# Modulation steps tied to TensorE's three waits at each LayerNorm boundary, and the two moment sums in a PSUM bank each

## The chip, the cores and the metric

The kernel runs on one core of one Trainium2 chip. Its engines are TensorE (PE in the profile; PEld is its weight load), VectorE (DVE), ScalarE (ACT), GpSimd (POOL) and SyncE (SP), which issues the loads. The metric is the device time of one execution in microseconds, the median of several runs.

## What is computed

One denoising step of a two-layer backbone in float32, for 128 context tokens and 256 latent tokens of width 1024. Each layer has three sub-layers: a SwiGLU feed-forward, a mixer (latent attention beside a gated recurrence, joined by one output product) and a second feed-forward. All three have the same frame:

```python
h = x * (1 + m[1]) + m[0]
x = layer_norm(ALPHA * x + 0.5 * m[2] * swiglu(h, w_up, w_down), ln_g, ln_b)
h = x * (1 + m[4]) + m[3]
y, aux = mixer(h)
x = layer_norm(ALPHA * x + m[5] * y, ln_g, ln_b)
h = x * (1 + m[7]) + m[6]
x = layer_norm(ALPHA * x + 0.5 * m[8] * swiglu(h, w_up2, w_down2), ln_g, ln_b)
```

The nine vectors `m` of a layer are the modulation: SiLU of a conditioning vector times a 1024 by 9216 matrix, once for the context tokens and once for the latent ones. They depend on no token, so their products can be done at any time before their first use; their weights are 72 MB in all.

## The kernel before

**Layout.** The residual stream `X` is kept transposed: eight chunks of 128 features on the partitions, 384 tokens along the free axis. A float32 product is made of three matmuls of reduced-precision parts (`mm3`, L317): a weight tile `ws` is split by ScalarE (`wh`, L313) and VectorE (`wl`, L314), the input by `split_affine` (L273) into `hh` and `hl`. Each of the three lines L318 to L320 is one 128x128 by 128x384 matmul.

**The modulation pump.** `Pump` cuts the modulation products into steps. One step takes a tile `wm` of 1 MB (three buffers, loaded by SP at L189). A group of `by_tensor` does a step as matmuls with 32 output rows on TensorE (L236); a group of `by_vector` sums on VectorE (L248, L250) and leaves a small matmul. When a group's last step is done, `finish` turns the result by a VectorE transpose (L228) and adds a bias (L229). `PUMPED` is the order of the groups, `MIX_STEPS` and `NEXT_STEPS` say how many steps are traced at the mixers and at the boundaries.

**The boundary.** `Residual.add` (L345) takes a finished output chunk `c`: two VectorE instructions put it into `X` (L349), ScalarE squares it (L354), GpSimd adds it to the running sums of values and of squares (L358, L359). At chunk 6 the sums so far go into PSUM by matmuls with a column of 1/1024 (`columns`, L373), one column a 128-token tile, the means and the mean squares side by side in one bank that a matmul with zeros has cleared (L362); another matmul spreads the mean over all partitions (`pm`, L367). At chunk 7 `moments` (L376) adds the last chunk to all of these (L373, L383); ScalarE squares the mean (L386), VectorE subtracts (L387), GpSimd takes the power -0.5 (L389). `normalise` (L392) transposes the roots into rows `pr` on TensorE (L396), and for each chunk VectorE subtracts and multiplies (L398, L399), after which `split_affine` makes the next input: ScalarE's `hh` (L276) in a context half and a latent half, `h32` by VectorE in even chunks and ScalarE in odd ones (L282, L279), VectorE's `hl` (L284). TensorE's next product needs both halves of `hh`'s first chunk. `next_input` (L451) ties this together for five boundaries; the sixth residual ends the kernel and has no next input.

**Order.** A scheduler orders each engine's instructions by the dependences, its own estimate of times, and a priority, which is the place in the program; `tc.high_priority(offset=n)` moves instructions n places forward. So a step that `next_input` traces may run much earlier or later. Each engine runs its instructions in the order that results. PSUM has three buffers for the small tiles (`misc_tile`: the moments, `pm`, `pr`) and one for the modulation.

## Time and profile before

| | before |
|---|---|
| median of 3 runs | 1615.8 us (1614.57 to 1617.2) |
| span of the profiled execution, first to last instruction | 1610.9 us |
| the profiled execution's own time beside its span | not recorded; the median of the runs stands 4.9 us above the span |
| TensorE busy | 1554.1 us (96% of the span) |
| VectorE, ScalarE, GpSimd busy | 948.3, 659.3, 163.0 us |
| mean granted TensorE clock | 0.984 of full speed |

The profile gives every instruction's start and duration from the start of the span. A row of the timeline names the start, the duration of a run of equal instructions, the engine, the line, the operation, what it writes and reads, and in brackets how long the engine idled before it and what ended that. One matmul of float32 operands stands as two records. Matmuls overlap, so a row's duration is longer than what the next one has to wait; 0.34 us is printed for a product matmul that follows the one before it by 0.17. The granted clock is a share of 2.4 GHz: 0.50 is the lower level, 1.2 GHz.

### The profile page before, as it was taken

The numbers are of one execution on the slowest core, as the hardware profiler recorded it, in microseconds if no ns is written. First come the engines' busy times: TensorE is split into PE (matmuls) and PEld (weight loads), VectorE is DVE, ScalarE is ACT, GpSimd is POOL, SyncE is SP. The second block draws the span as 40 slices with busy tenths as digits, with TensorE's granted clock in tenths as the row PEclk, the third lists the DMA queues.
The fourth block names the chain that finished last, engine by engine and source line by source line (L and its number), as shares of the span: only waits on it lengthen the run. The fifth ranks groups of instructions, "written<-read, shape, count | busy, mean of one in ns | idle before, by whom it ended". The sixth has DMA issues, their size and how long they took to land.

```text
span 1610.9 us, 22640 instructions
## 1 busy us (share of the span) xinstructions
PE 1554.1 (96%) x9106; PEld 1445.0 (90%) x9106; DVE 948.3 (59%) x1556; ACT 659.3 (41%) x1066; POOL 163.0 (10%) x142
## 2 busy tenths in 40 slices
PE   6999999999999899999999999999999989999997
PEld 3899999987668899999989999997867789999996
DVE  2868764477887846873464444345788664444334
ACT  3533333258743533332353333324785444333321
POOL 0000002220004100000220000032010140000012
PEclk8999999999999999999999999999999989999998
DMA  8865653446654545663354334334465214433331
GB/s 305 272 200 175 230 169 126 117 150 207 217 191 132 178 135 182 196 215 120 125 183 134 128 122 133 124 102 164 147 191 202 73 59 131 132 130 120 129 118 40
DMA packets 210596, 249.90 MB, mean 155 GB/s; under 512 B 26298, under 2 KB 185020, under 8 KB 207420
## 3 DMA queue, kind: packets, MB, share of 16 engines
q1 hardware_dynamic: 210492, 248.47, 46.8%
q8 instruction: 71, 1.16, 0.3%
q14 instruction: 33, 0.27, 0.1%
HBM read 245.52 MB, written 1.88 MB: 154 GB/s over the span
## 4 chain that ended last, share of the span: by engine, by line
PE 86%; DVE 5%; issue 3%; DMA 2%; ACT 2%; POOL 1%; SPq 0%; DVEq 0%; POOLq 0%; ACTq 0%
PE acc L318 26%; PE acc L319 26%; PE acc L320 26%; PE gm L236 3%; DMA wm<-in_w_mod_dram 2%; PE acc L745 1%; DVE wl L314 1%; PE ms L373 1%; PE pv L778 1%; PE ms L761 0%; ACT wh L313 0%; DVE hl L284 0%; POOL sum_f L359 0%; DVE tr L866 0%; SPq L189 0%
## 5 line engine op out<-in xcount | busy, mean ns | idle before, releaser
L313 ACT CAST wh<-ws 128x1024 fp32r<-128x1024 f32 (+1 forms) x330 | 335.7, 1019 | 778.3 <-PE acc L319 552.1
L314 DVE TENSOR_TENSOR wl<-ws,wh 128x1024 fp32r<-128x1024 f32 (+1 forms) x330 | 411.1, 1247 | 389.8 <-ACT wh L313 388.7
L318 PE MATMUL acc<-hh,wh 128*128 128x384 f32 x1280 | 428.8, 339 | 7.9 <-ACT hh L276 7.4
L320 PE MATMUL acc<-hh,wl 128*128 128x384 f32 x1280 | 431.9, 338 | 2.9 <-DVE wl L314 2.9
L319 PE MATMUL acc<-hl,wh 128*128 128x384 f32 x1280 | 431.6, 338 | 1.4 <-DVE hl L284 1.4
L318 PEld LDWEIGHTS acc<-hh,wh 128*128 128x128 f32 x1280 | 242.4, 190 | 15.5 <-ACT hh L276 9.0
L320 PEld LDWEIGHTS acc<-hh,wl 128*128 128x128 f32 x1280 | 242.6, 190 | 8.6 <-DVE wl L314 5.5
L319 PEld LDWEIGHTS acc<-hl,wh 128*128 128x128 f32 x1280 | 242.4, 189 | 7.6 <-DVE hl L284 4.4
L318 PE MATMUL acc<-gh,wh 128*128 128x384 f32 x704 | 236.6, 336 | 0.0
L319 PE MATMUL acc<-gl,wh 128*128 128x384 f32 x704 | 236.1, 335 | 0.0
L320 PE MATMUL acc<-gh,wl 128*128 128x384 f32 x704 | 235.9, 335 | 0.0
L318 PEld LDWEIGHTS acc<-gh,wh 128*128 128x128 f32 x704 | 132.2, 188 | 0.4 <-issue 0.4
L319 PEld LDWEIGHTS acc<-gl,wh 128*128 128x128 f32 x704 | 132.3, 188 | 0.0
L320 PEld LDWEIGHTS acc<-gh,wl 128*128 128x128 f32 x704 | 132.2, 188 | 0.0
L481 DVE TENSOR_TENSOR a<-a,acc 128x384 f32<-128x384 f32 x88 | 48.7, 554 | 126.2 <-PE acc L320 125.7
L250 DVE SCALAR_TENSOR_TENSOR gsum<-wm,sil,gsum 128x512 f32<-128x512 f32 x168 | 120.3, 766 | 0.0
L318 PE MATMUL acc<-hh_in,wh 128*128 128x384 f32 x352 | 118.0, 339 | 2.2 <-ACT hh_in L276 2.2
L320 PE MATMUL acc<-hh_in,wl 128*128 128x384 f32 x352 | 117.8, 335 | 0.7 <-DVE wl L314 0.7
L319 PE MATMUL acc<-hl_in,wh 128*128 128x384 f32 x352 | 118.2, 336 | 0.0
L358 POOL TENSOR_TENSOR sum_f<-X 128x384 f32<-128x384 f32 x4 | 5.1, 1282 | 846.3 <-DVE X L349 846.3
L236 PE MATMUL gm<-wm,sil 128*32 128x256 f32 (+1 forms) x512 | 66.2, 532 | 13.0 <-DMA wm<-in_w_mod_dram 11.9
L318 PEld LDWEIGHTS acc<-hh_in,wh 128*128 128x128 f32 x352 | 66.2, 189 | 4.5 <-ACT hh_in L276 3.2
(260 smaller groups left out, 1721.9 us busy)
## 6 DMA issues: line engine op xcount, KB each, us to landing
ws<-in_w_ffn_up_dram SPq DMA_DIRECT2D x88, 1024.0 KB, 5.2
wm<-in_w_mod_dram SPq DMA_DIRECT2D x56, 1024.0 KB, 6.8
ws<-in_w_ffn_down_dram SPq DMA_DIRECT2D x32, 1024.0 KB, 5.0
wm<-in_w_mod_dram SPq DMA_DIRECT2D x32, 512.0 KB, 5.8
ws<-in_w_ffn_down_dram SPq DMA_DIRECT2D x16, 768.0 KB, 4.4
ws<-in_w_in_dram SPq DMA_DIRECT2D x12, 1024.0 KB, 5.4
ws<-in_w_o_dram SPq DMA_DIRECT2D x8, 1024.0 KB, 8.5
ws<-in_w_uq_dram SPq DMA_DIRECT2D x12, 192.0 KB, 3.2
```

The lines of the kernel that those rows point to most:

```text
L236: nc.tensor.matmul(self.ps[32 * g : 32 * g + 32, :n], lhsT, wv[:, g], start=self.fresh, stop=stop)
L250: nc.vector.scalar_tensor_tensor(self.sum[:, r], wv[:, kk], s, self.sum[:, r], op0=ALU.mult, op1=ALU.add)
L313: nc.scalar.copy(parts[0], src)
L314: nc.vector.tensor_tensor(parts[1], src, parts[0].bitcast(F32), op=ALU.subtract)
L318: nc.tensor.matmul(ps, wh, xh, start=start, stop=False)
L319: nc.tensor.matmul(ps, wh, xl, start=False, stop=False)
L320: nc.tensor.matmul(ps, wl, xh, start=False, stop=stop)
L358: nc.gpsimd.tensor_tensor(self.sums[0], X[:, 0, :] if c == 1 else self.sums[0], X[:, c, :], op=ALU.add)
L373: nc.tensor.matmul(self.pt[:, 2 * i + j : 2 * i + j + 1], src[:, i * P : (i + 1) * P], mean_w[:, 0:1], start=False, stop=stop and i == T / ...
L481: nc.vector.tensor_tensor(a, a, px[:, :T], op=ALU.mult)
L745: nc.tensor.matmul(views[i], qT[hf][0:96, h % 4, q0 : q0 + P], kT[hf][0:96, h % 4, k0:k1], start=True, stop=True)
L778: nc.tensor.matmul(o[:, P:T], v, pTs[e][:, (j - 1) * 256 : j * 256], start=(j == 1), stop=(j == 3))
```

## The change

`next_input` no longer runs its steps at its start. It hands their number to `moments` and `normalise`, which place them by a new function `fill`: a step is traced at high priority, and each of its TensorE instructions is ordered behind a given one (`tc.issue_after`). The first step goes behind the last product's last matmul, the second behind the last column sum of squares, the remaining ones (one, or two at the third boundary) behind the transposes, which become high priority themselves.

The means and the mean squares get one PSUM bank each (two of the three small buffers at that time, so that `pm` takes the third and `pr` waits for the first to be free); each bank is cleared by a matmul with zeros of its own. The mean's column sums and `pm` come first; VectorE copies the mean out of PSUM and squares the copy, where ScalarE squared it; then the column sums of squares follow. In the first chunk of each boundary VectorE makes the context half of `hh` (`swift`). The last tensor group of two vectors, (1, 7) and (1, 8), becomes two groups of one. In the result's `finish` the copy of the mean is the one that `moments` makes. The rest of the diff removes comments.

```diff
@@ PUMPED
-          + by_vector((1, 1), (1, 3), (1, 4)) + by_tensor((1, 2)) + by_tensor((1, 5), (1, 6)) + by_tensor((1, 7), (1, 8)))
+          + by_vector((1, 1), (1, 3), (1, 4)) + by_tensor((1, 2)) + by_tensor((1, 5), (1, 6)) + by_tensor((1, 7))
+          + by_tensor((1, 8)))
@@ split_affine
-            nc.scalar.activation(hh[:, c, t0:t1], X[:, c, t0:t1], AF.Identity,
-                                 bias=B[:, c, r : r + 1], scale=G[:, c, r : r + 1])
+            if swift and r == 0:
+                nc.vector.tensor_scalar(hh[:, c, t0:t1], X[:, c, t0:t1], G[:, c, r : r + 1], B[:, c, r : r + 1],
+                                        op0=ALU.mult, op1=ALU.add)
+            else:
+                nc.scalar.activation(hh[:, c, t0:t1], X[:, c, t0:t1], AF.Identity,
+                                     bias=B[:, c, r : r + 1], scale=G[:, c, r : r + 1])
@@ mm3
-        nc.tensor.matmul(ps, wl, xh, start=False, stop=stop)
+        newest["product"] = nc.tensor.matmul(ps, wl, xh, start=False, stop=stop)
+
+    def fill(ins, n=1):
+
+        with tc.high_priority(offset=CHAIN_AHEAD), tc.issue_after(ins.ins):
+            pump.step(n)
@@ Residual.add
-                    self.pt = misc_tile()
-                    nc.tensor.matmul(self.pt[:, :6], mean_w, zeros, start=True, stop=False)
+                    self.pt = [misc_tile() for _ in range(2)]
                     for j in range(2):
+                        nc.tensor.matmul(self.pt[j][:, :3], mean_w, zeros[:, :3], start=True, stop=False)
                         self.columns(j, self.sums[j])
@@ moments
-        def moments(self):
+        def moments(self, fills=0):
+
             name = self.name
+            if fills:
+                fill(newest["product"])
             with tc.high_priority(offset=CHAIN_AHEAD):
-                self.columns(0, self.tail[0])
-                self.columns(1, self.tail[1], stop=True)
+                self.columns(0, self.tail[0], stop=True)
                 if self.broadcast:
                     nc.tensor.matmul(self.pm[:, :T], mean_w, self.tail[0], start=False, stop=True)
-                mv = self.pt[:, :6].rearrange("p (a b) -> p a b", b=2)
+                mean = tmp.tile([P, 4], F32, tag="v4", name=f"mean_{name}")
+                nc.vector.tensor_copy(mean[:, :3], self.pt[0][:, :3])
                 m2 = tmp.tile([P, 4], F32, tag="m2", name=f"m2_{name}")
-                nc.scalar.activation(m2[:, :3], mv[:, :, 0], AF.Square)
-                nc.vector.scalar_tensor_tensor(m2[:, :3], mv[:, :, 1], LN_EPS, m2[:, :3], op0=ALU.add, op1=ALU.subtract)
+                nc.vector.tensor_tensor(m2[:, :3], mean[:, :3], mean[:, :3], op=ALU.mult)
+                last = self.columns(1, self.tail[1], stop=True)
+                nc.vector.scalar_tensor_tensor(m2[:, :3], self.pt[1][:, :3], LN_EPS, m2[:, :3], op0=ALU.add, op1=ALU.subtract)
...
+            if fills > 1:
+                fill(last)
+            return mean, rs
@@ normalise
-            _, rs = self.moments()
+            _, rs = self.moments(fills)
             pm, pr = self.pm, misc_tile()
-            for i in range(3):
-                nc.tensor.matmul(pr[:, i * P : (i + 1) * P], rs[:, i : i + 1].to_broadcast([P, P]), ident, start=True, stop=True)
+            with tc.high_priority(offset=CHAIN_AHEAD):
+                for i in range(3):
+                    last = nc.tensor.matmul(pr[:, i * P : (i + 1) * P], rs[:, i : i + 1].to_broadcast([P, P]), ident,
+                                            start=True, stop=True)
+            if fills > 2:
+                fill(last, fills - 2)
@@ next_input
-        pump.step(steps)
         pump.finish()
...
-        for c in res.normalise():
-            split_affine(hh, hl, c, G, B)
+        for c in res.normalise(steps):
+            split_affine(hh, hl, c, G, B, swift=c == 0)
```

## Rows read from the trace of the kernel before

**Rows 1.** The page: its first line, and section 4's shares of the chain by engine.

```profile
span 1610.9 us, 22640 instructions
...
PE 86%; DVE 5%; issue 3%; DMA 2%; ACT 2%; POOL 1%; SPq 0%; DVEq 0%; POOLq 0%; ACTq 0%
```

**Rows 2.** Timeline, first boundary; [ ] is the engine's idle time before.

```profile
318.55 0.34 PE L320 MATMUL acc<-gh,wl 128*128 128x384 f32 x1
...
319.71 0.83 PE L373 MATMUL ms<-mean_w,sum_f 128*128 128x1 f32 x6 [0.26 <-POOL sum_f L359]
...
321.33 0.62 PE L236 MATMUL gm<-wm,sil 128*32 128x256 f32 x2
...
323.73 2.79 PE L236 MATMUL gm<-wm,sil 128*32 128x256 f32 x46
...
324.29 0.88 POOL L389 TENSOR_TENSOR r_f<-m_f,mhalf 128x3 f32<-128x3 f32 x1 [4.63 <-DVE m_f L387]
...
326.45 0.93 PE L396 MATMUL ms<-ident,r_f 128*128 128x128 f32 x6
...
329.44 1.10 PE L318 MATMUL acc<-hh,wh 128*128 128x384 f32 x3 [1.73 <-ACT hh L276]
```

**Rows 3.** Timeline, third boundary.

```profile
820.01 2.79 PE L236 MATMUL gm<-wm,sil 128*32 128x256 f32 x46
...
822.73 0.93 PE L396 MATMUL ms<-ident,r_f 128*128 128x128 f32 x6
...
824.29 1.37 ACT L276 ACTIVATE hh<-X,B,G 128x128 fp32r<-128x128 f32 x3 [4.00 <-DVE X L399]
824.64 0.66 DVE L282 TENSOR_SCALAR h<-X,G,B 128x128 f32<-128x128 f32 x2
...
825.33 0.79 PE L318 MATMUL acc<-hh,wh 128*128 128x384 f32 x3 [1.54 <-ACT hh L276]
```

**Rows 4.** Timeline, second boundary.

```profile
520.72 0.34 PE L320 MATMUL acc<-hh_mix,wl 128*128 128x384 f32 x1
...
520.99 1.06 PE L236 MATMUL gm<-wm,sil 128*32 128x512 f32 x8
...
529.52 0.79 PE L318 MATMUL acc<-hh,wh 128*128 128x384 f32 x3 [0.72 <-ACT hh L276]
```

**Rows 5.** Timeline, fourth boundary.

```profile
1101.98 0.34 PE L320 MATMUL acc<-gh,wl 128*128 128x384 f32 x1
...
1113.40 0.80 PE L318 MATMUL acc<-hh,wh 128*128 128x384 f32 x3 [1.73 <-ACT hh L276]
```

**Rows 6.** Timeline, fifth boundary.

```profile
1305.95 0.34 PE L320 MATMUL acc<-hh_mix,wl 128*128 128x384 f32 x1
...
1309.08 0.17 ACT L386 ACTIVATE m_m<-ms 128x3 f32<-128x3 f32 x1 [1.40 <-PE ms L373]
...
1310.44 1.65 PE L396 MATMUL ms<-ident,r_m 128*128 128x128 f32 x6 [1.40 <-POOL r_m L389]
...
1313.75 1.33 PE L318 MATMUL acc<-hh,wh 128*128 128x384 f32 x3 [1.67 <-ACT hh L276]
```

**Rows 7.** Windows, product matmuls: length, busy (records), clock, DMA share, GB/s.

```profile
329.44:343.00 13.56, 13.07 (x65) 0.87 0.33 141
825.33:839.00 13.67, 12.26 (x67) 1.00 0.59 231
...
1313.75:1328.00 14.25, 14.25 (x66) 0.79 0.00 1
529.52:543.00 13.48, 12.92 (x62) 0.87 0.24 84
300.00:313.00 13.00, 13.00 (x76) 1.00 0.59 151
```

**Rows 8.** Windows, attention: length; PE, PEld, DVE, ACT, POOL busy; clock, DMA, GB/s.

```profile
1220.00:1230.00 10.00, 9.93 (x52) 4.32 (x51) 8.92 (x23) 6.69 (x20) 0.00 (x0) 1.00 0.79 288
```

**Rows 9.** Loads of modulation weights (L189), from issue to landing.

```profile
DMA to landing us min/median/max: 3.7/6.5/12.4
```

More of the change, by code (lines that the diff above doesn't have):

```diff
@@ L271, in load_x, with split_affine @@
             nc.scalar.mul(X[:, c, :], ps[:, :T], ALPHA)
-    def split_affine(hh, hl, c, G, B):
+    def split_affine(hh, hl, c, G, B, swift=False):
         h32 = tmp.tile([P, T], F32, tag="t1", bufs=3, name=f"h32_{n_ps[0]}_{c}")
         for r, (t0, t1) in enumerate(COND):
-            nc.scalar.activation(hh[:, c, t0:t1], X[:, c, t0:t1], AF.Identity,
-                                 bias=B[:, c, r : r + 1], scale=G[:, c, r : r + 1])
+            if swift and r == 0:
[4 more added lines that the diff above has]
+                                     bias=B[:, c, r : r + 1], scale=G[:, c, r : r + 1])
             if c % 2:
@@ L315, in piece @@
         return parts
+    newest = {}
     def mm3(ps, wh, wl, xh, xl, start, stop):
@@ L372, in columns @@
             for i in range(T // P):
-                nc.tensor.matmul(self.pt[:, 2 * i + j : 2 * i + j + 1], src[:, i * P : (i + 1) * P], mean_w[:, 0:1],
-                                 start=False, stop=stop and i == T // P - 1)
-        def moments(self):
+                last = nc.tensor.matmul(self.pt[j][:, i : i + 1], src[:, i * P : (i + 1) * P], mean_w[:, 0:1],
+                                        start=False, stop=stop and i == T // P - 1)
+            return last
+        def moments(self, fills=0):
@@ L397, in normalise @@
+            return mean, rs
+        def normalise(self, fills):
+            _, rs = self.moments(fills)
+            pm, pr = self.pm, misc_tile()
+            with tc.high_priority(offset=CHAIN_AHEAD):
[4 more added lines that the diff above has]
+                fill(last, fills - 2)
             for c in range(KD):
@@ L424, in finish @@
         def finish(self, dsts):
-            mv, rs = self.moments()
-            mean = tmp.tile([P, 4], F32, tag="v4", name=f"mean_{self.name}")
-            nc.vector.tensor_copy(mean[:, :3], mv[:, :, 0])
+            mean, rs = self.moments()
             for i, dst in enumerate(dsts):
```

2 lines of the change are left out of this document (removed).

## The prediction

> **What bounds the kernel now.** I read the page first. The chain that ended last runs on TensorE for 86% of the span [rows 1], and most of that is products of 384 columns that nobody can shorten here; so a change can only pay where TensorE waits or runs slowly. I then asked the timeline for the five stretches between the last product of one sub-layer and the first of the next, numbered 1 to 5 in order of time. Stretch 1 takes 318.55 to 329.44 (10.9 us), 2 takes 520.72 to 529.52 (8.8), 4 takes 1101.98 to 1113.40 (11.4), 5 takes 1305.95 to 1313.75 (7.8); 3 ends at 825.33 [rows 2 to 6]. In each there are three waits of TensorE: for the last chunk's sum on VectorE, for the reciprocal root (GpSimd), and for the first normalised chunk.
>
> What the reader is to see in stretch 1 [rows 2]: the root is done at 324.29 + 0.88 = 325.17, but the transposes that need it start at 326.45, because 46 records of modulation (three steps of 16 less two records, 2.79 us) stand ahead of them in TensorE's order. The work meant to fill a wait outlasts it by 1.3 us. Behind the transposes TensorE then idles 1.73 us with nothing to fill. Stretch 3 has the same block of 46 at 820.01 [rows 3]. Stretch 5 has no modulation at all: its steps ran long before, in the attention.
>
> Last I read the clock, from windows that begin at each first product [rows 7]. Where stretch 3 ends the granted clock is 1.00; after 1 and 2 its mean over 13.5 us is 0.87 and after 5, over 14.25, it is 0.79, so part of those windows ran at the lower level, 1.2 GHz, and the rest at 2.4. In undisturbed products 76 records take 13.00 us, 0.171 us each. By that, what each window loses is: after 1, 13.56 - 65 x 0.171 = 2.4, less a piece of a step like the stray 0.62 of rows 2: 1.8; after 3, 13.67 - 67 x 0.171 = 2.2, less a step (1.06): 1.1; after 5, 14.25 - 66 x 0.171 = 3.0; after 2, 13.48 - 62 x 0.171 = 2.9. For 4, whose code is that of 1, I take 1's. Stretch 3 is the one whose TensorE kept its clock through the boundary; 1.1 us is what the start costs when VectorE and ScalarE deliver the chunks and the clock holds.
>
> **The change part by part.** *Steps tied to the waits.* One step behind the last product, one behind the column sums of squares, the rest behind the transposes. A step is 1.06 us [rows 4]. In the three stretches behind a feed-forward (1, 3, 4) the first step goes ahead of the column sums, where TensorE is itself the chain: +1.06. Against that, stretch 1 loses a wait of 0.26 and the 0.62 of stray modulation [rows 2]; with the 0.2 of the next part the root then ends where it does now, 325.15, but only one step (1.06) stands in a wait of some 1.3, so the transposes start at once: 326.45 - 325.15 = 1.3 us won. Stretch 3 has the same block: 1.3. Stretch 4 is the same code as 1, so I give it the same length afterwards (below). Behind a mixer (2, 5) the first step starts as the last product ends, while the columns wait for VectorE anyway; I count it as free.
>
> *Mean and squares in two banks.* The mean is copied out and squared on VectorE while TensorE still sums the squares; ScalarE's square, 0.17 and a handover [rows 6], leaves the chain: 0.2 us at each. The new copy and product are two three-column VectorE instructions; the nearest row, that ScalarE square of the same shape, is 0.17, and both have the sums of squares as cover. If that cover is gone they cost 0.2 to 0.35 at each. The product reads two SBUF operands, and here the Trainium skill speaks against it ("SBUF — State Buffer", section "Who interferes with whom"): such a VectorE instruction can be blocked by a GpSimd instruction that reads SBUF. No GpSimd instruction overlaps it in rows 2, the root at 324.29 being the next; were one there, as long as that one (0.88), the sum would be 5 x 0.9 = 4.4 us poorer, 1605. The second bank needs one more clearing matmul at six places; three matmuls of the column sums take 0.83 [rows 2], so 0.28 each, 1.7 in all if nothing covers them and nothing in the waits: I take half, -0.8.
>
> *First chunk's first half on VectorE.* ScalarE's three pieces take 1.37 [rows 3], some 0.45 each; one leaves the path, 0.4. VectorE's two pieces of the same kind take 0.66, so 0.33 are added there, beside ScalarE's second piece and hidden by it; uncovered they eat 0.3 of the 0.4.
>
> *Stretches added up.* 1: 1.3 + 0.4 = 1.7, so 9.2 long. 3: 1.7. 4, at 9.2: 11.4 - 9.2 = 2.2. For 5, the transposes there took 1.65 against 0.93 in stretch 1 (they ran at the lower clock) [rows 2, 6]: 0.7 + 0.2 + 0.4 = 1.3, so 6.5 long; 2 at the same length: 8.8 - 6.5 = 2.3. Together 9.2 us.
>
> *Clock behind them.* The third step runs in the wait before the first product (1.73 us idle in stretch 1). I take it that the clock then holds as in stretch 3, whose idle stretch before its first product was about as long (transposes end 823.66, product 825.33 [rows 3]) but whose TensorE had just run 2.8 us of modulation; that is the weakest step. Worth, against 1.1: 0.7 + 1.8 + 0.7 + 1.9 = 5.1 us. Lower bound nothing.
>
> *Steps leaving the attention.* Stretch 5 gets three steps that now run in the attention, around 1220 to 1230 for the most part, where TensorE is 99% busy [rows 8]. 3 x 1.06 = 3.2 at most, nothing at least, since there they may fill small waits; I take half, 1.6.
>
> *The rest.* Splitting the last pair of vectors into two groups keeps the number of steps and bytes (eight steps of 1 MB); it lets the factors of stretch 5 be ready before the steps tied into it. Finishing a group on VectorE (transpose and add) now falls into the start after 2, as today, and after 5, where it is new: up to 0.6 estimated from the two VectorE pieces of 0.66, kept for the range. The loads of the tied steps move forward in SP's queue with them; ahead of them are only weights already on their way, behind them the next sub-layer's first weights. The end of the kernel only loses the 0.2 of the square.
>
> Sum: 9.2 + 5.1 + 1.6 - 0.8 = 15.1. The profiled execution's span, 1610.9 [rows 1], becomes 1595.8. Its own time outside the span was not recorded; the median of the runs, 1615.8, stands 4.9 above the span, and I carry this over: 1600.7, say **1601 us**.
>
> **The rivals.**
> *The waits are filled but the clock is not held.* For it: the drop behind 1 follows an idle stretch no longer than that of 3. Then 5.1 and the 0.7 of stretch 5 are lost, and the attention may give nothing (1.6), the clearing matmuls their full price (0.9 more): 15.1 - 8.3 = 6.8, 1609.
>
> *No change to speak of.* The steps only change places: the first, tied ahead of the column sums, delays the chain by as much as the second and third win, and the clock falls as before. What stays is 5 x (0.2 + 0.4) = 3.0 less 0.8: 1613.6. Against it stands the 1.3 us block in stretches 1 and 3, which nothing but order causes.
>
> *Slower: a tied step waits for its weights.* TensorE works in order, so a step whose megabyte has not landed holds the transposes or the products behind it, whereas today it can stand elsewhere. The place is stretches 2 and 5, whose steps follow the mixer's 14 and 10 through three buffers. A load lands in 6.5 us, 3.7 to 12.4 [rows 9]; less a step's 1.06 of cover that is 5.4 each, 33 for six: 1616 + 33 - 15 = 1634. It decides from 15.1 / 6 = 2.5 us a step. Against it: in stretch 2 two steps ran with no wait for a load before 520.99 [rows 4], and after the attention the whole output product is left to load in. The skill's page "TensorE: Matmul & The Clock Gate" (section "Step-by-step: what each phase is for") says that matmuls stay in program order; the 46 records ahead of transposes that were ready show it here.
>
> **How the numbers follow.** Forecast as summed 0.62; clock not held 0.18; no change 0.10; late loads 0.10. Some 0.2%, 3.2 us, is what a measurement of this kernel can tell from no change. So faster 0.80, same 0.10, slower 0.10. The range: downwards the attention's full 3.2 (1.6 more), free clearing matmuls (0.8) and starts that lose less than stretch 3's 1.1 (5 x 1.1 = 5.5): 1593, with rounding 1592. Upwards the first rival's 1609 and a part of one late load (5.4): 1613. It leaves out the last part of the second rival and the third.
>
> **What would show it.** Right: in stretch 1 about 16 records of modulation between the last product and the column sums, 16 between the sums of squares and the transposes, 16 after; transposes within 0.1 us of the root; first product about 9.2 us after the last in 1 and 4, 6.5 in 2 and 5; no ScalarE square; clock 1.00 in windows of 13.6 us after each first product. Wrong: an idle of TensorE ended by a load of modulation inside a stretch; a clock of 0.87 still; the first chunk waiting on VectorE's transposes of a finished group; or the column sums waiting on the added clearing.

## The result, and the profile after

The changed kernel takes 1631.26 us (1628.43 to 1634.27, 4 runs) against 1615.18 (1614.21 to 1617.2, 4 runs): ratio 1.009, 95% interval 1.0065 to 1.0114. It is slower; 1601 was predicted, with a range that ends at 1613. The page after, its first line, chain by engine, and one group of section 5:

```profile
span 1631.8 us, 22814 instructions
...
PE 85%; DVE 7%; issue 4%; ACT 2%; DMA 1%; POOL 1%; SPq 0%; POOLq 0%; DVEq 0%; ACTq 0%
...
L326 PE MATMUL acc<-hl,wh 128*128 128x384 f32 x1280 | 432.9, 338 | 5.0 <-DVE hl L289 4.9
```

Beside [rows 1], the one share of the chain that grew by more than a point is VectorE's, 5% to 7%, and the wait that stands out in the list is TensorE's for `hl`, the second part of the normalised chunks, which VectorE makes (5.0 us; 1.4 before).

Two windows of each boundary tell where the time went: the **gap**, from the start of the last product to that of the first, and the **ramp**, from there to the start of the 144th product matmul of the next sub-layer. Columns: window, its length, busy time and instructions of each engine, mean granted clock, DMA share. After, in pairs of gap and ramp, boundary 1 first (in the second pair from 531.31, third from 825.09, and so on):

```profile
322.11:334.20 12.09, 12.09 (x87) 7.75 (x87) 6.18 (x16) 2.92 (x6) 1.98 (x2) 0.72 0.57 190
334.20:365.31 31.11, 30.73 (x173) 25.27 (x171) 26.24 (x59) 17.45 (x35) 7.46 (x10) 1.00 0.51 181
...
531.31:540.30 8.99, 7.71 (x48) 3.56 (x48) 6.06 (x16) 2.74 (x5) 0.86 (x1) 1.00 0.60 200
540.30:570.81 30.51, 26.88 (x145) 24.93 (x146) 30.37 (x53) 18.20 (x32) 8.45 (x8) 1.00 0.54 184
825.09:834.21 9.12, 8.91 (x86) 5.97 (x86) 5.66 (x15) 2.45 (x5) 1.96 (x2) 1.00 0.66 224
834.21:864.50 30.29, 28.61 (x164) 25.21 (x163) 21.48 (x40) 16.75 (x32) 6.57 (x8) 1.00 0.49 178
1114.10:1125.77 11.67, 11.67 (x64) 6.59 (x63) 5.66 (x15) 2.41 (x5) 1.97 (x2) 0.71 0.74 249
1125.77:1157.38 31.61, 30.70 (x171) 25.19 (x168) 26.10 (x57) 17.97 (x37) 8.56 (x10) 1.00 0.54 192
1325.72:1335.05 9.33, 8.25 (x71) 4.44 (x70) 6.15 (x16) 2.75 (x5) 0.86 (x1) 1.00 0.31 86
1335.05:1363.27 28.22, 26.52 (x143) 24.57 (x144) 20.20 (x36) 18.09 (x32) 7.89 (x8) 1.00 0.37 123
```

The same windows before, the ramps of boundaries 1 and 2, both windows of 3, the ramps of 4 and 5:

```profile
329.45:357.46 28.01, 28.01 (x154) 26.54 (x154) 23.19 (x54) 17.50 (x35) 8.50 (x10) 0.94 0.34 120
...
529.51:561.33 31.82, 29.37 (x143) 27.80 (x144) 30.20 (x53) 18.78 (x33) 6.82 (x8) 0.89 0.42 137
814.83:825.33 10.50, 8.71 (x86) 6.29 (x86) 6.87 (x16) 2.69 (x6) 1.96 (x2) 1.00 0.59 200
825.33:852.38 27.05, 26.57 (x159) 25.08 (x160) 18.90 (x36) 16.85 (x32) 6.89 (x8) 1.00 0.55 197
...
1113.40:1142.68 29.28, 29.24 (x154) 25.93 (x155) 23.51 (x53) 17.73 (x35) 8.51 (x10) 0.94 0.41 150
...
1313.75:1342.98 29.23, 28.34 (x143) 27.25 (x144) 21.12 (x35) 18.78 (x33) 6.41 (x8) 0.90 0.24 74
```

Boundary 3 is the cleanest: the clock is 1.00 in all four windows. Its gap fell from 10.50 to 9.12, 1.4 of the 1.7 predicted, and its ramp grew from 27.05 to 30.29. The first product came earlier, and the 144th later, by 39.41 - 37.55 = 1.9 us.

To add up windows of different clocks I take from each length half of the time that it ran at 1.2 GHz (what TensorE would have needed at 2.4 GHz; an estimate where another engine sets the length). So counted, the five gaps went from 47.2 to 44.4, the five ramps from 135.7 to 151.7, all the rest of the span from 1401.9 to 1400.6: +12.0, so counted all of it in the ramps. The other 8.8 of the 20.9 us between the two spans is clock: 52.4 us at 1.2 GHz before, 70.0 after. As they ran, the gaps grew by 1.8, the ramps by 6.4 and the rest by 12.7, for before much of the time at 1.2 GHz lay in the ramps and after it lay outside them. Whether the count takes too much off a ramp that VectorE paces can be seen at boundary 4: before, that ramp ran 29.28 and counts as 27.57; with the two banks alone (below), where the last `hl` of that boundary ends 0.1 us earlier (22.93 against 23.04), it ran at 1.00 throughout and took 27.74.

Over all runs of this study the span times its mean clock, a number that counts in the same way, is 1586.5 for the kernel before (98 runs, standard deviation 1.3) and 1596.4 after (4 runs, 0.8): +9.9; the time at 1.2 GHz, twice the rest of the span, rose from 56 to 66, which is +5.0. Both terms are clear of the spread, and the larger is not the clock's.

**What is late in the ramp.** Boundary 3 after, TensorE:

```profile
825.09 0.34 PE L327 MATMUL acc<-gh,wl 128*128 128x384 f32 x1
825.36 1.07 PE L237 MATMUL gm<-wm,sil 128*32 128x256 f32 x16
...
829.12 0.81 PE L397 MATMUL ms<-X,mean_w 128*128 128x384 f32 x2
829.76 0.73 PE L385 MATMUL ms<-mean_w,sq_f 128*128 128x1 f32 x6
830.42 1.05 PE L237 MATMUL gm<-wm,sil 128*32 128x256 f32 x10
831.68 0.93 PE L415 MATMUL ms<-ident,r_f 128*128 128x128 f32 x6 [0.21 <-POOL r_f L405]
832.54 1.50 PE L237 MATMUL gm<-wm,sil 128*32 128x256 f32 x22
...
834.21 0.77 PE L325 MATMUL acc<-hh,wh 128*128 128x384 f32 x3
```

and VectorE in the same boundary, first after, then before:

```profile
830.03 0.55 DVE L420 TENSOR_TENSOR X<-X,ms 128x384 f32<-128x384 f32 x1 [1.78 <-PE ms L397]
830.52 0.16 DVE L403 SCALAR_TENSOR_TENSOR m_f<-ms,m_f 128x3 f32<-128x3 f32 x1
830.60 1.01 DVE L420 TENSOR_TENSOR X<-X,ms 128x384 f32<-128x384 f32 x2
832.65 1.02 DVE L421 TENSOR_TENSOR X<-X,ms 128x384 f32<-128x384 f32 x2 [1.04 <-PE ms L415]
...
848.97 0.56 DVE L289 TENSOR_TENSOR hl<-h,hh 128x384 fp32r<-128x384 f32 x1 [1.85 <-ACT h L284]
```

```profile
819.63 0.55 DVE L398 TENSOR_TENSOR X<-X,ms 128x384 f32<-128x384 f32 x1 [2.24 <-PE ms L383]
820.33 0.16 DVE L387 SCALAR_TENSOR_TENSOR m_f<-ms,m_f 128x3 f32<-128x3 f32 x1
820.40 2.40 DVE L398 TENSOR_TENSOR X<-X,ms 128x384 f32<-128x384 f32 x5
823.71 1.02 DVE L399 TENSOR_TENSOR X<-X,ms 128x384 f32<-128x384 f32 x2 [0.90 <-PE ms L396]
...
836.74 0.56 DVE L284 TENSOR_TENSOR hl<-h,hh 128x384 fp32r<-128x384 f32 x1 [1.10 <-ACT h L279]
```

The change did to TensorE what the diff says: one step behind the product, 10 records between the squares and the transposes, transposes within 0.2 us of the root. But look at VectorE. Before, while TensorE ran its block of 46 records [rows 3], VectorE subtracted the mean from six of the eight chunks (1 + 5). After, the transposes come sooner, the multiplications are ready sooner, and three subtractions are done (1 + 2); the other five stand between the chunks later, where VectorE pauses for 0.25 us in all until its last multiplication. The last `hl` ends 24.44 us after the last product instead of 22.47. The "overrun" of 1.3 us that the prediction booked as a gain was VectorE's working time.

That explains why nothing was won, but not yet the loss. At this boundary VectorE idles as long ahead of its first multiplication in both kernels (0.90 and 1.04 in the rows), so three early subtractions less cost it nothing by themselves. Of the 1.97 us, 0.15 are a later start, 0.96 more VectorE work up to the last `hl`, 0.75 the longer wait ahead of that `hl` for ScalarE (1.85 against 1.10), and the rest small pauses. Over all five boundaries the last `hl` ends 11.2 us later, by the same reading of the two traces: VectorE starts 0.5 earlier, idles 4.1 more between its first subtraction and its first multiplication and 2.3 more later on, and works 5.3 more (of which 1.2 for the half chunk that it took from ScalarE, 1.0 each in `h32` and in `hl`, 1.9 in finished modulation groups and small pieces). Most of the 4.1 lies at boundaries 1 and 4, where the clock fell inside the gap (at 4 VectorE idles 1.1 there before and 2.8 after).

### The profile page after: what moved, and what is told of

It is laid out like the page before. It is cut to its first block, busy times and chain, and to the rows that moved or that the text cites. A ratio compares the mean times of both kernels' runs of the same rounds, so it can differ in the third digit from the quotient of the medians.

```text
span 1631.8 us, 22814 instructions
## 1 busy us (share of the span) xinstructions
PE 1571.7 (96%) x9182; PEld 1452.1 (89%) x9182; DVE 953.5 (58%) x1572; ACT 656.1 (40%) x1055; POOL 161.8 (10%) x142
## 4 chain that ended last, share of the span: by engine, by line
PE 85%; DVE 7%; issue 4%; ACT 2%; DMA 1%; POOL 1%; SPq 0%; POOLq 0%; DVEq 0%; ACTq 0%
PE acc L325 26%; PE acc L326 25%; PE acc L327 25%; PE gm L237 3%; PE acc L764 1%; DVE wl L319 1%; DMA wm<-in_w_mod_dram 1%; DVE hl L289 1%; PE ms L385 1%; PE pv L797 1%; PE ms L780 1%; DVE h L287 1%; ACT wh L318 0%; DVE tr L885 0%; DVE X L421 0%
## 5 line engine op out<-in xcount | busy, mean ns | idle before, releaser
L251 DVE SCALAR_TENSOR_TENSOR gsum<-wm,sil,gsum 128x512 f32<-128x512 f32 x168 | 116.9, 746 | 0.0
L237 PE MATMUL gm<-wm,sil 128*32 128x256 f32 (+1 forms) x576 | 69.4, 511 | 13.6 <-DMA wm<-in_w_mod_dram 12.5
```

What stands on the lines that cost most here:

```text
L237: nc.tensor.matmul(self.ps[32 * g : 32 * g + 32, :n], lhsT, wv[:, g], start=self.fresh, stop=stop)
L251: nc.vector.scalar_tensor_tensor(self.sum[:, r], wv[:, kk], s, self.sum[:, r], op0=ALU.mult, op1=ALU.add)
```

## The experiments

The theories named in the expectations: A, VectorE's work from the mean's spread (`pm`) to the last `hl` sets the length of a boundary, and the first product does not; B, the time is lost where steps left the mixers; C, in the first two, the two banks and VectorE's added work cost it. That it is the clock alone is what the count at full clock answers. Each kernel has its median beside the kernel before on the same chip (1615.9 to 1617.0), and the ratio with its interval; "full clock" is the span times the mean clock over all its runs, 1586.5 for before and 1596.4 for after.

**Parts of the change undone.** *No ties:* the steps are traced at the start of `next_input` again; the transposes keep their priority.

```diff
+        pump.step(steps)
         pump.finish()
...
-        for c in res.normalise(steps):
+        for c in res.normalise(0):
```

> The changed kernel with the ties taken out: the modulation steps are traced at the start of each boundary again, as before the change; the two banks, VectorE's square of the mean, the first half chunk on VectorE and the split of the last group stay. Theory A (VectorE sets the length of a boundary, from the spread of the mean to the last chunk of the next input, and the tied steps delay its start and make it wait): the last chunk is ready 21.5 to 23.5 us after the last product again, 1612 to 1620 us. Theory B (steps that left the mixers cost there, by the clock): the two mixers get their steps back, also 1612 to 1620, but with boundaries as long as in the changed kernel. Rival C (the two banks and the added VectorE work cost the time): 1626 to 1634.

1620.56, 1.0018 (1.0002 to 1.0034), full clock 1590.6. Most of the loss goes with the ties, 4 us of it do not; the time is just above the forecast of A and B and well below that of C. The last `hl` came into the expected 21.5 to 23.5 us at two boundaries of five.

*Ties alone,* on the kernel before: steps tied, transposes at high priority, the last pair of vectors in two groups; one bank, no faster half.

```diff
+            if fills:
+                fill(newest["product"])
...
+            if fills > 1:
+                fill(last)
...
+            if fills > 2:
+                fill(last, fills - 2)
```

> The kernel before with nothing but the ties (and the split of the last group that they need, and the transposes of the roots at high priority): one bank, ScalarE's square and ScalarE's first half chunk as before. Theories A and B: 1624 to 1634 us, like the changed kernel. Rival C: 1612 to 1618.

1636.16, 1.0115 (1.0097 to 1.0133), full clock 1600.4, the slowest order of all. With one bank the order that came out put the mean's spread behind the transposes at boundaries 1, 3 and 4; at 3:

```profile
829.09 1.65 PE L409 MATMUL ms<-ident,r_f 128*128 128x128 f32 x6
...
831.25 0.91 PE L393 MATMUL ms<-X,mean_w 128*128 128x384 f32 x2
```

There VectorE cannot subtract before 9.6 to 11.1 us after the last product (4.8 in the changed kernel at 3), and the last `hl` is 18.7 us later over five boundaries than before. So this run shows what a late spread costs, and is no clean test of the ties.

*No step ahead of the column sums;* it joins the ones behind the transposes:

```diff
-            if fills:
-                fill(newest["product"])
...
-                fill(last, fills - 2)
+                fill(last, fills - 1)
```

> The changed kernel with no step behind the last product: that step moves behind the transposes. Theory A: the mean's spread ends 0.8 to 1.1 us earlier at the boundaries behind a feed-forward (three of them) and not at the others, and the last chunk is ready that much earlier: 3 us less than the changed kernel, 1626 to 1630. Theory B: unchanged within its runs, 1628 to 1634.

1619.32, 1.0017 (1.0003 to 1.0031), full clock 1586.9: this alone brings all 9.5 us at full clock back, three times the 3 us of theory A (1626 to 1630). The gaps came down to 40.2 (44.4 after), and the ramps to 146.5.

*The first step alone,* on the kernel before:

```diff
-        pump.step(steps)
+        fill(newest["product"])
+        pump.step(steps - 1)
```

> The kernel before, with one step of each boundary tied behind the last product as in the change, the others where they were, and the last pair of vectors split into two groups as in the change; no second bank, no transposes at high priority. If the change lost its time because this step pushes the mean's spread back and VectorE starts late, the spread ends some 1 us later at each boundary, the last hl follows by about 1 us, and the product of span and clock grows by 3 to 6 us: 1619 to 1623. If the first step alone is harmless and only its meeting with few early subtractions costs, the 46-record block that covers VectorE's subtractions stays about as long and the growth is under 2 us: 1617 to 1618.

1615.4, 0.9991 (0.9974 to 1.0008), full clock 1585.3. The step that costs 9.5 us in the changed kernel costs nothing in the kernel before: the other steps still stand ahead of the transposes, and 3 to 6 subtractions are done under them. So it is not this step, but the step together with transposes that no longer wait: here VectorE's first subtractions start 1.9 us later in all, and it idles 2.1 less ahead of its first multiplications.

*Transposes early alone,* on the kernel before, all steps of a boundary tied behind them:

```diff
-        pump.step(steps)
...
+            with tc.high_priority(offset=CHAIN_AHEAD):
                 for i in range(3):
...
+            fill(last, fills)
```

> The kernel before with the one part from which the prediction drew its largest gain: the transposes at high priority and all steps of a boundary tied behind them (the last pair of vectors in two groups, as in the change); one bank, no step ahead of the transposes. By the prediction, first products 1.3 us earlier at boundaries 1, 3 and 4 and the time 4 to 6 us lower. By what the runs so far show, the block of modulation hid VectorE's subtractions: first products 1.3 to 1.9 us earlier at those boundaries, the last hl not earlier by more than 0.3 us, and the product of span and clock within 1.5 us of 1586.4.

1619.68, 1.0027 (1.0011 to 1.0043), full clock 1589.8: the part from which the largest gain was forecast makes the kernel slower. Boundary 3, TensorE and then VectorE:

```profile
823.48 0.93 PE L402 MATMUL ms<-ident,r_f 128*128 128x128 f32 x6 [1.40 <-POOL r_f L394]
824.34 2.80 PE L237 MATMUL gm<-wm,sil 128*32 128x256 f32 x48
```

```profile
822.41 1.01 DVE L406 TENSOR_TENSOR X<-X,ms 128x384 f32<-128x384 f32 x2
824.45 1.02 DVE L407 TENSOR_TENSOR X<-X,ms 128x384 f32<-128x384 f32 x2 [1.04 <-PE ms L402]
```

Two subtractions are done before the first multiplication, where six were. The expectation by theory A, within 1.5 us of the kernel before at full clock, is missed too. The gaps are 3.1 us shorter at full clock, the ramps 8.7 longer.

*Two banks alone* (the changed moments; no ties, no faster half, transposes and groups as before):

```diff
+                nc.vector.tensor_copy(mean[:, :3], self.pt[0][:, :3])
...
-                nc.scalar.activation(m2[:, :3], mv[:, :, 0], AF.Square)
...
+                nc.vector.tensor_tensor(m2[:, :3], mean[:, :3], mean[:, :3], op=ALU.mult)
```

> The kernel before with the moments alone as in the change: two banks, the mean copied and squared on VectorE, the sums of squares last. By the prediction's terms 0.2 us won at each boundary less some clearing matmuls: no change, 1616 to 1617. If this part holds what is left of the loss when the ties are taken out (product of span and clock 1590.6 against 1586.4 before), the product comes out near 1590 and the time at 1619 to 1621.

1617.08, 1.0006 (0.9988 to 1.0023), full clock 1586.2: nothing, as the prediction's 5 x 0.2 - 0.8 said.

*No faster half* in the changed kernel:

```diff
-            split_affine(hh, hl, c, G, B, swift=c == 0)
+            split_affine(hh, hl, c, G, B)
```

> The changed kernel with the first half of the first chunk back on ScalarE. By the prediction's term of 0.4 us at each boundary the kernel gets 2 us slower: about 1633. If VectorE's work sets the boundary, 0.33 us leave VectorE at each and the kernel gets 1 to 2 us faster, about 1630; a difference this small shows in the product of span and clock (1596.4 for the changed kernel) and not in the median.

1626.95, 1.0058 (1.0036 to 1.0079), full clock 1592.9: 3.5 us less than with it, where the prediction had it winning 2 and theory A costing 1 to 2. The 0.34 us piece stands on VectorE, and five of them are 1.7 at most; the rest is not accounted for.

*Steps of boundaries 2 and 5 in the mixers again:*

```diff
-NEXT_STEPS = (3, 3, 4, 3, 3)
-MIX_STEPS = (14, 10)
+NEXT_STEPS = (3, 0, 4, 3, 0)
+MIX_STEPS = (17, 13)
```

> The changed kernel with the three steps each of boundaries 2 and 5 traced at the mixers again, none tied at those two boundaries. If the time is lost because these steps left the mixers (the mixers' products took 163.3 and 163.3 us before, 166.0 and 168.3 after), both stretches come back to about 163.3 and the total falls by some 8 us against the changed kernel, to about 1623. If VectorE's work sets each boundary (from the mean's spread to the last chunk's second part), only boundaries 2 and 5 change, by 1 to 2 us each, the mixers vary by a few us with their lower-clock stretches, and the total stays at 1626 to 1631.

1625.49, 1.006 (1.0039 to 1.0081), full clock 1593.2, 3.2 under the changed kernel, and between the two forecasts (1623 by B, 1626 to 1631 by A). Against theory B: outside gaps and ramps this kernel needs 1406.8 at full clock, 6.2 more than the changed one; its gain comes from gaps and ramps (9.3 less).

**VectorE's load changed.** *All subtractions ahead of the first multiplication,* in the changed kernel:

```diff
             for c in range(KD):
                 nc.vector.tensor_tensor(X[:, c, :], X[:, c, :], pm[:, :T], op=ALU.subtract)
+            for c in range(KD):
                 nc.vector.tensor_tensor(X[:, c, :], X[:, c, :], pr[:, :T], op=ALU.mult)
```

> The changed kernel with all eight subtractions of the mean traced ahead of the first multiplication, so that VectorE has work while it waits for the transposes. Theory A: VectorE's idle time in front of the first multiplication (1.0 to 2.3 us) goes, the last chunk is ready 1 to 2 us earlier at each of five boundaries though TensorE's first product may start later: 1621 to 1627. Theory B or a TensorE-bound boundary: no gain or a loss of up to 2 us a boundary, 1631 to 1641.

1618.5, 1.0014 (0.9999 to 1.0029), full clock 1586.6, better than theory A's 1621 to 1627. At boundary 3 the second to eighth subtractions now run in one piece:

```profile
822.64 3.33 DVE L420 TENSOR_TENSOR X<-X,ms 128x384 f32<-128x384 f32 x7
```

This settles which mark counts: the first products come 8.4 us later than before over five boundaries and 6.6 later than in the changed kernel, the last `hl` 9.6 earlier than there, and the loss is gone. VectorE keeps working while the root is made: its idle time ahead of the first multiplications falls from 9.0 to 3.4 us over the five.

*Each `hl` made twice,* on the kernel before:

```diff
         nc.vector.tensor_tensor(hl[:, c, :], h32, hh[:, c, :].bitcast(F32), op=ALU.subtract)
+        nc.vector.tensor_tensor(hl[:, c, :], h32, hh[:, c, :].bitcast(F32), op=ALU.subtract)
```

> The kernel before, with VectorE's subtraction that makes hl issued twice for every chunk at the boundaries (the same values written again): eight instructions of about 0.55 us, 4.4 us of VectorE, at each. If VectorE sets a boundary's length, each of the five grows by 3 to 4.4 us (144th product 3 to 4.4 us later), 15 to 22 us in all, 1632 to 1639. If TensorE sets it, with the first product as the mark, the work hides beside the products: 0 to 4 us, 1617 to 1621.

1648.22, 1.019 (1.0157 to 1.0223), full clock 1605.0. With 5 x 4.4 = 22 us more VectorE work it is 18.5 slower at full clock, and 80 us ran at 1.2 GHz against 56. So VectorE's work at a boundary is on the path, in the kernel before too. How much of it is less clear: in the order that came out here the ramps also hold 9 us more of modulation on TensorE than before (at 1.06 us a step, an estimate), so not all of the 18.5 need be VectorE's.

*`h32` of chunks 2 and 6 from VectorE to ScalarE,* on the kernel before:

```diff
-            if c % 2:
+            if c % 4:
```

> The kernel before, with the h32 halves of chunks 2 and 6 made by ScalarE: four VectorE pieces of 0.33 us, 1.3 us, leave VectorE at each boundary. If VectorE sets a boundary's length, the last hl comes 1.0 to 1.3 us earlier and the 144th product 0.7 to 1.3 us, 4 to 6.5 us in all: 1610 to 1613. If TensorE sets it, or ScalarE is as late as VectorE, no change: 1615 to 1618.

1617.81, 1.0012 (0.9996 to 1.0028), full clock 1586.4: nothing won, and theory A had promised 4. VectorE's last multiplication is 7.2 us earlier over the five boundaries, the last `hl` only 2.7. ScalarE is late next; at boundary 3 VectorE waits 1.20 us for its last piece:

```profile
835.43 0.56 DVE L284 TENSOR_TENSOR hl<-h,hh 128x384 fp32r<-128x384 f32 x1 [1.20 <-ACT h L279]
```

So A has to be mended: with VectorE relieved ScalarE is the later one, and what goes with the ramp is the last `hl`, whoever is late for it.

*Three at once:* the changed kernel with no first step, subtractions first, and `if c % 4`.

> The changed kernel without the step tied behind the last product (it joins the ones behind the transposes), with all eight subtractions of the mean ahead of the first multiplication, and with the h32 halves of chunks 2 and 6 on ScalarE. If VectorE sets a boundary's length: the mean's spread is back at 4.0 us after the last product, VectorE works without a pause from there, the last hl is 1 to 1.5 us ahead of before's, the 144th products sum to 187 to 191 us against 194.8, and the total is 1609 to 1613, under the kernel before. If TensorE sets it: 1618 to 1620, as each of the two undoings alone gave.

1617.04, 0.9999 (0.9988 to 1.001), full clock 1586.4. All of the loss is undone and nothing more is won, where theory A had promised 1609 to 1613. As in the run before, VectorE waits for ScalarE: behind its last multiplications it idles 12.5 us over the five boundaries (4.6 before).

*`h32` of chunks 2 and 6 on GpSimd,* on the kernel before and on the changed one:

```diff
+            if c in (2, 6):
+                nc.gpsimd.tensor_scalar(h32[:, t0:t1], X[:, c, t0:t1], G[:, c, r : r + 1], B[:, c, r : r + 1],
+                                        op0=ALU.mult, op1=ALU.add)
-            if c % 2:
+            elif c % 2:
```

> The kernel before, with the h32 halves of chunks 2 and 6 made by GpSimd, which is idle for most of a boundary: the 1.2 us a boundary that leave VectorE as in the run that gave them to ScalarE, but ScalarE keeps its load. If VectorE and ScalarE together set the last hl, it comes 0.7 to 1.2 us earlier at each boundary, and the time falls by 3 to 5 us, to 1612 to 1614. If GpSimd's pieces hold VectorE up, or come late themselves (a GpSimd instruction of this kind over a whole chunk took 0.90 us), no gain or a loss: 1617 or more.

> The changed kernel with the h32 halves of chunks 2 and 6 on GpSimd. If VectorE's work behind the mean's spread is what its loss comes from, the last hl comes 1 to 1.5 us earlier at each boundary and the product of span and clock falls from 1596.4 to 1590 or 1592. If the loss has another place (the mixers, loads), it stays above 1595.

On the kernel before: 1613.14, 0.9976 (0.996 to 0.9992), faster by a quarter of a per cent and within the forecast; full clock 1584.9, so that 1.6 of the 2.9 us are not clock. On the changed kernel: 1625.21, 1.0054 (1.0038 to 1.007), full clock 1594.7, 1.7 less than without. That second step is less than A forecast (1590 to 1592): the last `hl` moved 5.2 us over five boundaries and gaps and ramps shrank by 5.9, but in its one profile the rest of the span was 4.1 longer. I did not find out why.

*The last chunk's `h32` on VectorE,* which waits there with nothing to do, and chunk 6's on ScalarE instead, on the kernel before; then the same with chunks 2 and 5 on GpSimd:

```diff
-            if c % 2:
+            if c in (1, 3, 5, 6):
```

> The kernel before with the h32 of chunk 7 made by VectorE and that of chunk 6 by ScalarE, an exchange. VectorE's last subtraction waits 1.1 us for ScalarE's last h32 piece while it has nothing else to do. If the last hl sets the time, it comes 0.6 to 1.0 us earlier at each boundary and the time falls by 2 to 4 us. If not: no change.

```diff
+            if c in (2, 5):
+                nc.gpsimd.tensor_scalar(h32[:, t0:t1], X[:, c, t0:t1], G[:, c, r : r + 1], B[:, c, r : r + 1],
+                                        op0=ALU.mult, op1=ALU.add)
-            if c % 2:
+            elif c in (1, 3, 6):
```

> The kernel before with h32 of chunks 0, 4 and 7 on VectorE, 1, 3 and 6 on ScalarE, 2 and 5 on GpSimd: both VectorE and ScalarE lose one chunk's halves, and the last one no longer comes from ScalarE. If the last hl sets the time, it comes 1.2 to 2 us earlier at each boundary and the time falls by 4 to 7 us, to 1609 to 1612. If TensorE is the limit by then, as little as the run with two chunks on GpSimd gave: 1613.

1614.34, 0.9994 (0.9979 to 1.0009), full clock 1582.9; and 1612.2, 0.9977 (0.9959 to 0.9994), full clock 1583.0. At full clock the exchange wins 3.6 us; in the median of the first it is lost in the clock (60 us at 1.2 GHz). The second beats both kernels, by 3.7 and 19 us in the median, just short of the forecast 4 to 7; at full clock it is level with the exchange alone. At boundary 3 of the first, the last wait is no longer for an `h32` (the last `hl` is not earlier at this one, and 0.9 to 1.5 us earlier at the other four):

```profile
839.78 0.62 DVE L284 TENSOR_TENSOR hl<-h,hh 128x384 fp32r<-128x384 f32 x1 [0.32 <-ACT hh L276]
```

**All together.** For each kernel, from its one profiled execution: five first products and five last `hl` ends, us after the last product, summed; gaps, ramps and the rest of the span at full clock; and the full-clock time over all its runs.

```
                    first    last                                all
                  product      hl     gap    ramp     rest      runs
before               49.4   113.1    47.2   135.7   1401.9    1586.5
after                51.2   124.3    44.4   151.7   1400.6    1596.4
no ties              50.7   118.4    45.2   142.0   1403.4    1590.6
ties alone           57.5   131.9    52.1   149.6   1396.9    1600.4
no first step        45.4   113.5    40.2   146.5   1403.3    1586.9
first step alone     50.7   113.4    47.2   137.2   1401.0    1585.3
transposes early     51.0   117.6    44.1   144.4   1403.0    1589.8
two banks alone      50.4   113.9    49.0   134.3   1402.6    1586.2
no faster half       51.3   121.4    44.5   148.8   1400.9    1592.9
steps in mixers      45.5   119.6    39.3   147.5   1406.8    1593.2
subtractions first   57.8   114.7    54.4   130.6   1402.9    1586.6
hl twice             51.3   138.8    45.8   158.4   1399.6    1605.0
h32 to ScalarE       48.4   110.5    46.0   136.6   1404.3    1586.4
three at once        56.5   117.0    47.9   135.6   1402.2    1586.4
h32 to GpSimd        54.2   113.1    50.8   130.8   1403.8    1584.9
after, GpSimd        52.9   119.1    44.3   145.9   1404.8    1594.7
last h32 swapped     48.9   108.7    48.3   132.3   1400.7    1582.9
swapped, GpSimd      50.9   108.7    50.6   130.1   1401.8    1583.0
```

Over these 18 kernels the full-clock time goes with the last `hl` (correlation 0.97, 0.76 us for each us) and not with the first product (0.16). With the ratios of the medians, from which no clock is taken off, it is 0.95 and 0.10. Gaps tend to be short where ramps are long (correlation -0.58).

One rival is left by such a correlation. TensorE's own modulation work inside the ramps differs too: at 1.06 us a step (an estimate) 3.0 us before and 6.6 after, and over the 18 kernels it goes with the full-clock time almost as well (0.90). Two readings speak against it as the cause. At boundary 3 the ramp holds 16 records of modulation in both kernels and still grew by 3.2 us; and the changed kernel with GpSimd's pieces has 3.4 us of it, near the 3.0 of the kernel before, and is 8.2 us slower at full clock. It may be a part of the 16.1 us at boundaries 1 and 4, where 10 records became 26 and 24.

Where VectorE's time up to the last `hl` goes, for the kernels that part the theories (us over five boundaries; idle "ahead" is between the first subtraction and the first multiplication):

```
                    start of first   idle    idle            last
                     subtraction    ahead   later    work     hl
before                   24.8        4.9     5.0     78.4   113.1
after                    24.3        9.0     7.3     83.7   124.3
no first step            18.1        7.3     4.5     83.5   113.5
first step alone         26.7        2.8     4.9     79.1   113.4
transposes early         21.6        6.1     8.0     82.0   117.6
subtractions first       23.4        3.4     7.8     80.0   114.7
```

No single column makes the loss: one run takes it back by an earlier start, another by less idle time ahead.

## Why the prediction was wrong

*What bounds the kernel.* The chain named TensorE for 86%, and the prediction concluded that a change pays where TensorE waits. Inside a boundary that was the wrong reading of a right number: in the kernel before VectorE works with next to no pause at boundary 3 from the first multiplication until it waits 1.1 us ahead of the last `hl`, and TensorE, busy as it looks, goes at the rate at which chunks arrive (the run with all subtractions first bears this out).

*Steps tied to the waits.* At boundary 3 it went as forecast (first product 1.4 us earlier, 1.7 predicted; transposes 0.2 after the root). At 1 and 4 the gap grew to 12.09 and 11.67 (9.2 predicted), because the clock fell inside it: in the kernel with steps in the mixers again boundary 4 has the changed code, kept 1.00, and took 8.99, with its last `hl` at 24.06 us instead of 26.66 (23.04 before). At 5 the first step, "free" in the prediction, was not: the mean's spread ends 3.47 us after the last product instead of 2.53, the root starts at 5.59 instead of 3.58, since the step's records also stand in pairs between the columns. Gap 9.33, 6.5 predicted.

*Two banks.* Right: forecast at +0.2 for all, measured at nothing that can be told from the spread. *First chunk's half on VectorE.* Wrong in sign: 0.4 won at each was forecast, 3.5 us in all lost, in the changed kernel.

*Stretches added up.* **This step failed.** It sums lengths from the last product to the first and takes for granted that what is won there stays won. The gaps did get shorter, by 2.8 of the 9.2 (at full clock; as they ran they grew by 1.8); but the ramps behind them got 16.1 longer (6.4 as they ran), and the only term that the sum has for them is the clock's, a gain. The missing quantity is VectorE's way from the mean's spread to the last `hl`: when it starts, how long it idles and how much it has to do. It ended 11.2 us later over the five boundaries, by 4.1 of idle time ahead of the first multiplications, 2.3 of later idle time and 5.3 of more work, less 0.5 of an earlier start. Fewer early subtractions (6 before, 3 after at boundary 3) are a sign of it and not a price by themselves.

*Clock behind them.* The forecast of the clock came true and the gain did not: all five ramps run at 1.00 (0.94, 0.89, 1.00, 0.94, 0.90 before), but at full clock each of the five is longer, by 1.9 to 4.8 us, and even as they ran only those of 2 and 5 got shorter (31.82 to 30.51, 29.23 to 28.22). The 1.1 us that a start costs "when VectorE and ScalarE deliver the chunks" was read at boundary 3, where six subtractions were already done, and carried to a kernel in which three are. That this is what spoilt the figure is argued, not shown. And the time at 1.2 GHz went elsewhere: 23.9 us in gaps and ramps before, 13.7 after; 28.5 outside before, 56.4 after.

*Steps leaving the attention.* 1.6 was forecast; the rest of the span fell by 1.2 at full clock, and with those steps back it rose by 6.2. The sign is right, and its nearness in size is no proof: it is within what this rest varies by (1396.9 to 1406.8 over the table).

*The rivals.* That it ends slower was in the list, at 1634 and a tenth, for late loads. In the list of TensorE's waits no load stands between a last product and a 144th product at any of the five boundaries; the longest are for `hl` (1.4 at boundary 2) and for the weights' second part (1.2). So that rival got the side right by another mechanism. No rival had VectorE. One of the prediction's own signs did show, and small: at boundary 2 TensorE's first product waits 0.6 us for VectorE's end of a modulation group.

*What stays open.* The parts do not add: the first tied step costs 9.5 in the changed kernel and nothing in the kernel before, early transposes alone 3.3, the faster half 3.5 in the changed kernel. The table of VectorE's time shows how they join: a later start costs nothing as long as VectorE would have idled ahead of the roots anyway. Why the sum has just this size is not shown; the fall of the clock at boundaries 1 and 4, 2.6 us of the last `hl` at 4, is a part of it that other executions of the same kernel need not have. Nor is it settled why the changed kernel spends 10 us more at 1.2 GHz over its runs; the kernel with `hl` twice, which also waits more in its ramps, spends 24 more.

## What to carry to other kernels

When a fill "overruns" the wait it was put into, look at what the other engines do under it before booking the overrun as a gain. Where a product starts on chunks that another engine makes, the mark is the last chunk, not the first product: write down when the last one is ready, which engines it goes through, and how far each is from its limit. And when two engines share that work, taking load off one gains only what the other has to spare. Look first at who waits for whom at the tail of the last chunk: here an exchange of two pieces won 3.6 us at full clock, and giving pieces to the third engine (GpSimd) 1.6, and nothing on top of the exchange.

## What the runs showed of the hardware

The clock fell inside a boundary although TensorE had work. After, boundary 1, windows with the clock as the third column from the end:

```profile
322.11:326.10 3.99, 3.99 (x38) 2.93 (x38) 2.53 (x6) 1.49 (x2) 1.11 (x1) 1.00 0.66 198
326.10:332.90 6.80, 6.80 (x33) 4.17 (x35) 2.36 (x6) 0.13 (x1) 0.88 (x1) 0.50 0.60 216
```

The mean's spread, which took 0.81 at boundary 3, takes 1.49 here, ten records of a step 1.91 against 1.05, the transposes 1.65 against 0.93, although the engine had run products until 322.11, then a step and column sums. At boundary 3, with the same instructions, the clock stayed at 1.00; before, at boundary 1, it stayed there until 329.70, 11.15 us behind the last product. What decides between the two was not found.

GpSimd and VectorE held each other up. After, boundary 3, VectorE and then GpSimd, which rescales `X` there:

```profile
840.99 0.56 DVE L289 TENSOR_TENSOR hl<-h,hh 128x384 fp32r<-128x384 f32 x1
...
842.71 0.86 DVE L289 TENSOR_TENSOR hl<-h,hh 128x384 fp32r<-128x384 f32 x1
```

```profile
841.06 1.12 POOL L478 TENSOR_SCALAR X<-X,ag 128x384 f32<-128x384 f32 x1 [2.87 <-ACT h L284]
842.50 0.67 POOL L478 TENSOR_SCALAR X<-X,ag 128x384 f32<-128x384 f32 x1 [0.32 <-DVE h L287]
```

The first `hl` starts 0.07 us ahead of GpSimd's piece: `hl` takes 0.56 and the piece 1.12. The second starts 0.21 us behind one: `hl` takes 0.86 and the piece 0.67. In the boundaries of all 18 profiles 238 of 758 `hl` took over 0.7 us, and each of them began while a GpSimd piece was running; of the 203 that began up to 0.5 us ahead of one, none took more than 0.56.

The Trainium skill's page "SBUF — State Buffer" (section "Who interferes with whom") says that a VectorE instruction with two SBUF inputs, as `hl` is, contends with a GpSimd instruction that reads SBUF. The trace agrees, with 0.56 and 0.86 us.

So the meeting of the two is a part of VectorE's work at a boundary: 14 of the 40 `hl` took over 0.7 us before, 18 after, 23 with the transposes early and 5 with the subtractions first. The `h32` pieces on GpSimd did not add to it: with them on the kernel before 6 of 40 were long, and the mean was 0.60 us against 0.66. The product of the mean with itself, for which the prediction counted this as a risk, took 0.15 to 0.16 us at each boundary.
